# Six weight slabs of the forgetting attention split in halves ahead of time, and the relative bias written per head

## The chip, the cores and the metric

The kernel runs on one core of one Trainium2 chip. The metric is device time in microseconds (us) of one execution. A core has a matrix engine (PE), a vector engine (DVE), an activation engine (ACT) and a general engine (POOL), a sync engine (SP) that issues most of its transfers in order, and 16 DMA engines that move data between the chip's DRAM and the on-chip buffers.

## The reference, cut to what matters

Two transformer blocks run over 512 tokens of width 1024, in float32.

```python
# block 1
h = rmsnorm(x, ln1); z = h @ w_in
y_pool = pool_mixer(u_pool)                 # trailing means, widths 2, 4, 8, 16
y_gla  = gla_mixer(gq, gk, gv, gg, ga)      # chunked gated linear attention, 4 heads
y_fox  = fox_mixer(fq, fk, fv, ff)          # softmax(q k^T/8 + F_t - F_s) v, causal, 8 heads
x = x + concat(y_pool, y_gla, y_fox) @ w_o
x = x + (silu(h2 @ w_gate) * (h2 @ w_up)) @ w_down     # h2 = rmsnorm(x, ln2), inner width 2816
x = rmsnorm(x, ln_f)
# block 2
h = rmsnorm(x, norm_g); q_lat, c_kv, ..., z_a, z_b, gate_a, gate_b = split(h @ w_in)
y_a = mla_attention(...) * silu(z_a)        # latent attention, 8 heads
y_b = dsa_attention(...) * silu(z_b)        # top-128 keys of an index score, bias by relative position
x = x + (sigmoid(gate_a) * (y_a @ w_o_a) + sigmoid(gate_b) * (y_b @ w_o_b)) @ w_out
return rmsnorm(x, final_g)
```

## The kernel before

**Number format.** Every float32 operand of a product is kept as a high part and a low part in the matrix engine's rounded float32. `split` makes the two: ACT copies the operand with rounding into hi (L189), and DVE or POOL subtracts hi from it into lo (L191). A product is three matmuls into one bank: hi by hi, hi by lo, lo by hi.

**Weights.** A slab is a 128x1024 weight tile of 512 KB. `weight` loads it raw into tag `wr` (2 buffers) on SP's queue (L199) and splits it into tags `wh` and `wl` (3 buffers each). The lo of a slab goes to POOL or to DVE by `self.share`: with 1 all go to POOL, with 2 every second one. `ready` gives a slab: if it has been stored before in split form, it loads hi and lo from DRAM and no engine works on it; otherwise it calls `weight`.

**Stages and their times in the trace.** Linear attention with pooling and the first projections (`gla_phase`) runs from about 24 to 129 us. Forgetting attention (`fox_phase`) with the first half of `w_o` runs from 129 to about 217, and the second half of `w_o` to 242. The MLP has two halves of eleven gate/up steps and eight down steps each: gate/up 242 to 364, down 364 to 428, gate/up 428 to 553, down 553 to 614. Block 2 has its index and latent projections from 614, the latent attention from 680 to 797, the sparse attention to 982, then the output projections to 1050.

**Order.** The order of PE's work is written by hand in the program. A planner (`spawn`, `later`, `go`, `need`) keeps a clock of PE's work, counted as moving columns at 2.4 per ns. A thread yields the time until it wants to run again, and work that was put off with `later` (projections, `w_o`) fills the time between. The other engines run their own instructions in order, and so does SP's queue: a transfer that waits holds back those behind it.

**Linear attention.** Temporaries [128x512] come from tag `b` with 18 buffers, which are given out in turn. `gla_phase` uses them for its chains and for `pooling` (the `nx` tiles, L780 to L793), and the forgetting attention uses them for q and k (L815, L817), the split stacks of a head (`stacks`, L342 to L349) and the scores. Head 0 makes four tiles for its stacks and its output before its first score.

**Forgetting attention.** Pairs of heads p = 0 to 3 need the slabs fq p and fk p of `w1s`. The products `w_o` of half 0 need slabs `w1o` 0 to 3. All of these pass through `weight`.

**MLP.** The gate/up weights come through `weight`. Beside them, `store` takes one slab of block 2 per step from the list `ahead`: raw load into `sr` (2 buffers, L252), hi on ACT into `sh` (1 buffer), lo on POOL into `sl` (1 buffer), and two stores to DRAM (L259). `down` loads its weights as 704 KB tiles `wd` (2 buffers, L906) and splits them on ACT and DVE. `store` runs in every gate/up step from the second on and in the odd down steps. `relative` makes the relative bias in down steps 0 and 1 of half 0: two small matmuls, eight rows `gd` to DRAM, and one transfer of 2560 KB (L890) that writes each head's 640 values 128 times, each row one element further on. Block 2 reads it as the shear tensor, head by head.

**Block 2.** `attention` divides a score row by its sum either on DVE (L406, for the query blocks in `norm`) or on ACT (L408). For the sparse attention `norm` is `NDSA`. `merge_a(m)` loads 256 KB of gate_a into a buffer of tag `z` (3 buffers, L1254), multiplies it with the product (L1258) and sends it to DRAM tile `ma` from POOL's queue (L1215); gate_b uses the same tag.

Of the kernel before, what the change touches and what calls it, by code (L numbers as in the profile page):

```python
# [11 lines left out]
F32 = mybir.dt.float32  # L12
F32R = mybir.dt.float32r
# [7 lines left out]
P = 128  # L21
T = 512
D = 1024
KD = D // P
# [9 lines left out]
XR = 7  # L34
XO = 4
RSW = 800
LSW = 3000
RRW = 3300
KTW = 800
# [39 lines left out]
NS = 3  # L79
NFOX = (1, 3)  # L80
NMLA = ()
NDSA = (0,)
UNIT = 5120.0


class Body:
# [109 lines left out]

    def weight(self, src, n=1024, pool=None):
        raw = self.wp.tile([P, 1024], F32, tag="wr", name="wr", bufs=WR)
        self.nc.sync.dma_start(raw[:, :n], src)  # L199
        hi = self.wp.tile([P, 1024], F32R, tag="wh", name="wh", bufs=3)  # L200
        lo = self.wp.tile([P, 1024], F32R, tag="wl", name="wl", bufs=3)
        self.nw += 1
        if pool is None:
            pool = self.nw % self.share == 0
        self.split(hi[:, :n], lo[:, :n], raw[:, :n], self.nc.gpsimd if pool else self.nc.vector)
        return hi, lo
# [31 lines left out]
    def ready(self, name, i, n=1024):  # L238

        if (name, i) not in self.stored:  # L240
            return self.weight(self.A[name][i], n)
        out = []
        for tag, src in zip(("wh", "wl"), self.stored[name, i]):
            out.append(self.wp.tile([P, 1024], F32R, tag=tag, name=tag, bufs=3))
            self.nc.sync.dma_start(out[-1][:, :n].bitcast(F32), src)
        return out

    def store(self, pool, name, i, n=1024):

        nc = self.nc  # L250
        raw = pool.tile([P, 1024], F32, tag="sr", name="sr", bufs=2)[:, :n]
        nc.sync.dma_start(raw, self.A[name][i])  # L252
        hi, lo = (pool.tile([P, 1024], F32R, tag=t, name=t, bufs=1)[:, :n] for t in ("sh", "sl"))
        with self.tc.issue_after(self.last_split):
            self.split(hi, lo, raw, nc.gpsimd)
        self.stored[name, i] = kept = []
        for part, src in (("h", hi), ("l", lo)):
            kept.append(self.dp.tile([P, n], F32, name=f"{part}_{name}_{i}"))
            nc.sync.dma_start(kept[-1], src.bitcast(F32))  # L259

    def token_major(self, act, t, w):

# [314 lines left out]
    def w_o(self, mix, m, half):  # L577
        x = self.x[m]
        if m % 2 == 0:
            self.w_pair = self.weight(self.A["w1o"][half * 4 + m // 2])  # L580
        ps = yield from self.dense(self.w_pair, mix[4 * half:4 * half + 4], kt=4, w0=(m % 2) * 512)
        self.nc.vector.tensor_tensor(x, ps, x, op=OP.add)

    def gla_phase(self, ctx, h, R, Rc, mix, mp, b, fd, psg, held, V, proj):
        nc, A = self.nc, self.A
# [187 lines left out]
        def pooling(f):  # L773
# [22 lines left out]
            self.mm(ps, wpool[:, f, :], nx)  # L796
            self.split_scaled(mix[f][0], mix[f][1], ps, self.gain("pool_scale", f))

        self.spawn(chain(0, held))
        self.later("gv", gla_v(), 2 * UNIT)  # L800
        self.spawn(chain(1), CH1)
# [72 lines left out]
    def relative(self, pool):  # L874

        nc = self.nc
        relb = self.const(pool, "relb", [32, 8])
        onehot = self.const(pool, "onehot", [32, 640])
        shear = self.shear = self.dp.tile([8, P * 641], F32, name="shear")
        gd = self.dp.tile([8, 640], F32, name="gd")  # L880
        g8 = pool.tile([8, 640], F32, name="g8")
        yield
        for c in range(0, 640, 320):
            ps = self.bank("tr")
            self.mm(ps[:8, :320], relb, onehot[:, c:c + 320])
            nc.scalar.activation(g8[:, c:c + 320], ps[:8, :320], AF.Copy, scale=-1.0)
        nc.sync.dma_start(gd, g8)

        dst = bass.AP(tensor=shear.tensor, offset=shear.offset, ap=[[P * 641, 8], [641, P], [1, 640]])
        nc.sync.dma_start(dst, bass.AP(tensor=gd.tensor, offset=gd.offset, ap=[[640, 8], [0, P], [1, 640]]))  # L890
        yield

    def mlp(self, ctx):
        nc, A, x = self.nc, self.A, self.x
        fp = self.pool(ctx, "ff")
        wd = self.pool(ctx, "wd")
        act = [tuple(fp.tile([P, T], F32R, name=f"f{c}{k}") for c in "hl") for k in range(FH)]
        lng = fp.tile([P, KD], F32, name="lng")
        o, o2 = GAINS["ln_f"][0], GAINS["norm_g"][0]
        nc.vector.tensor_tensor(lng, self.gains[:, o:o + KD], self.gains[:, o2:o2 + KD], op=OP.mult)  # L900
        ft = lambda tag: fp.tile([P, T], F32, tag=tag, name=tag, bufs=2)
        self.res = self.dp.tile([T, D], F32, name="res")

        def down(m, half):
            raw = wd.tile([P, FH * P], F32, tag="wd", name="wd", bufs=2)
            nc.sync.dma_start(raw, A["w1d"][half * KD + m])  # L906
            hi, lo = (wd.tile([P, FH * P], F32R, tag=t, name=t, bufs=2) for t in ("wdh", "wdl"))
            self.split(hi, lo, raw)
            return hi, lo

        def turn(m):

            s, o = ft("g"), ft("u")
            nc.scalar.activation(s, x[m], AF.Identity, scale=self.gain("ln_f", m))
            yield
            tr = self.bank("tr")
            for t in range(NT):
                self.tp(tr[:, t * P:(t + 1) * P], s[:, t * P:(t + 1) * P])
            nc.scalar.activation(o, tr, AF.Copy)
            nc.sync.dma_start(self.res[:, m * P:(m + 1) * P].rearrange("(t p) c -> p t c", p=P),  # L920
                              o.rearrange("p (t c) -> p t c", c=P))

        t2 = lambda name, a, b: [("w2s", T2[name] + i, 1024) for i in range(a, b)]
        ahead = [("w2m", 0, KD * 72)] + t2("c_kv", 0, 2) + t2("q_idx", 0, 2) + t2("q_lat", 0, 3) + [("w2kv_v", 0, 1024)]
        ahead += t2("gate_b", 0, 8) + [("w2uq_r", 0, 768), ("w2pair", 0, 640)]
        for p in range(4):
            ahead += t2("gate_a", 2 * p, 2 * p + 2 if p < 2 else 4) + t2("z_a", p, min(p + 1, 3))
            ahead += [("w2pair", p + 1, 640)] if p < 2 else []
        ahead = deque(ahead)
        relative = self.relative(wd)  # L930
        turns = []
        for half in range(2):
            for k in range(FH):
                m = half * FH + k
                if m == 0:
                    self.entry()
                ps = self.first.pop(0) if self.first else self.all(self.dense(self.slab("w1gu", 2 * m), self.h))
                gen = None if self.first else self.dense(self.slab("w1gu", 2 * m + 1), self.h)
                g = ft("g")
                nc.vector.tensor_tensor(g, ps, self.R2, op=OP.mult)  # L940
                nc.scalar.activation(g, g, AF.Silu)
                ps = self.first.pop(0) if gen is None else self.all(gen)
                u = ft("u")
                nc.vector.tensor_tensor(u, ps, self.R2, op=OP.mult)  # L944
                nc.vector.tensor_tensor(u, u, g, op=OP.mult)
                self.split(act[k][0], act[k][1], u)
                if m and ahead:
                    self.store(wd, *ahead.popleft())
            for m in range(KD):
                ps = self.all(self.dense(down(m, half), act, kt=FH))  # L950
                if m % 2 and ahead:
                    self.store(wd, *ahead.popleft())
                if half == 0 and m < 2:
                    next(relative)
                nc.vector.tensor_tensor(x[m], ps, x[m], op=OP.add)  # L955
                if half == 1:
                    if m == 0:
                        h = self.acts()
                        s1, s2 = self.sums(), self.sums()
                    self.split_scaled(h[m][0], h[m][1], x[m], lng[:, m:m + 1])  # L960
                    eng = nc.vector if m == KD - 1 else nc.gpsimd
                    self.square_into(s1, x[m], m == 0, eng=eng)
                    self.square_into(s2, x[m], m == 0, scale=self.gain("ln_f", m), eng=eng)
                    for g in turns:
                        self.all(g)
                    turns = [turn(m)]
                    next(turns[0])
        self.s1, self.s2 = [s1], [s2]
        self.h, self.turns = h, turns
# [25 lines left out]
    def block2(self, ctx, psm, psc):  # L995
# [254 lines left out]
        wa = {}  # L1250

        def merge_a(m):
            g = at("z", 3)
            nc.sync.dma_start(g, kept["gate_a", m])  # L1254
            if m % 2 == 0:
                wa[0] = self.weight(A["w2oa"][m // 2])
# [297 lines left out]
```

## Time and profile before

| | |
|---|---|
| median of 3 runs | 1057.81 us (1057.36 to 1058.91) |
| profiled execution, its time | 1059.3 us |
| its span in the profile | 1057.4 us |
| PE busy | 1038.4 us, 98% |
| DVE, ACT, POOL busy | 641.7, 548.1, 371.2 us |
| PE's granted clock | 0.999 of 2.4 GHz |

The span runs from the first to the last instruction, and 1.9 us of the profiled execution's time lie around it. PE's busy time is what matmuls occupy by the profile; their ends are modelled.

### The profile page before, as it was taken

The page shows a single profiled execution, that of the slowest core. Times are in us where ns is not written, and L with a number is a line of the kernel's source. Part 1 is how long each engine was busy: PE and PEld are TensorE (multiplying, and loading weights), DVE is VectorE, ACT ScalarE, POOL GpSimd, SP SyncE. Part 2 cuts the span into 40 slices and gives each one's busy share as a digit, 9 for nine tenths or more (in the row PEclk, how much of TensorE's full clock was granted, in tenths as well). Part 3 has the DMA queues.
Part 4 walks back from the last instruction along what each step waited for, and adds up shares of the span by engine and source line. Part 5 has one row for each costly group of instructions (what it writes and reads, how often), then busy time and mean ns, then how long its engine had stood idle before and what let it go on. Part 6 is the DMA issues. An engine that isn't in the chain of part 4 may idle for free.

```text
span 1057.4 us, 14279 instructions
## 1 busy us (share of the span) xinstructions
PE 1038.4 (98%) x5264; PEld 862.3 (82%) x5264; DVE 641.7 (61%) x1141; ACT 548.1 (52%) x956; POOL 371.2 (35%) x213
## 2 busy tenths in 40 slices
PE   9999999999999999999999999999999999999997
PEld 6888977788888877888888888888887898888786
DVE  6573488866554522445434435799995656787652
ACT  7673578745433322243325545655565657677333
POOL 1243322133454522255433411100023346665354
PEclk9999999999999999999999999999999999999999
DMA  6222132226677588466776344564532323435842
GB/s 224 90 81 81 60 100 71 71 80 223 202 242 254 200 286 275 159 224 217 247 255 223 106 146 160 178 214 163 175 126 100 100 71 120 130 100 162 285 141 80
DMA packets 57822, 169.78 MB, mean 161 GB/s; under 512 B 6744, under 2 KB 11240, under 8 KB 57752
## 3 DMA queue, kind: packets, MB, share of 16 engines
q1 hardware_dynamic: 54664, 162.54, 45.9%
q10 hardware_dynamic: 2448, 4.22, 1.1%
q0 software_dynamic: 640, 2.10, 0.5%
q8 instruction: 42, 0.69, 0.3%
q14 instruction: 28, 0.23, 0.1%
HBM read 130.86 MB, written 40.60 MB: 162 GB/s over the span
## 4 chain that ended last, share of the span: by engine, by line
PE 54%; DMA 4%; ACT 2%; DVE 2%; issue 1%; SPq 1%; POOL 1%; DVEq 0%; POOLq 0%; ACTq 0%
PE mm L152 45%; PE sc L152 4%; PE pv L152 2%; PE tr L159 2%; DMA wd<-in_w1d 1%; PE tr L152 1%; DMA ma<-z 1%; SPq L252 1%; DMA l_w2s<-sl 1%; POOL sl L191 1%; DMA z<-gate_a 0%; DMA wl<-l_w2s 0%; DVE kst L191 0%; DVE qst L343 0%; ACT s L403 0%
## 5 line engine op out<-in xcount | busy, mean ns | idle before, releaser
L152 PE MATMUL mm<-hh,wh 128*128 128x512 f32 (+2 forms) x808 | 322.5, 399 | 0.2
L191 POOL TENSOR_TENSOR wl<-wr,wh 128x1024 fp32r<-128x1024 f32 (+1 forms) x78 | 195.2, 2504 | 362.6 <-ACT wh L189 340.0
L152 PE MATMUL mm<-hl,wh 128*128 128x512 f32 (+3 forms) x808 | 314.7, 389 | 0.9 <-DVE hl L527 0.9
L152 PE MATMUL mm<-hh,wl 128*128 128x512 f32 (+1 forms) x800 | 312.0, 390 | 0.0
L189 ACT ACTIVATE wh<-wr 128x1024 fp32r<-128x1024 f32 (+2 forms) x114 | 118.8, 1043 | 174.4 <-PE mm L152 145.9
L152 PEld LDWEIGHTS mm<-hh,wh 128*128 128x128 f32 (+1 forms) x808 | 152.0, 188 | 30.9 <-issue 1.3
L152 PEld LDWEIGHTS mm<-hh,wl 128*128 128x128 f32 (+1 forms) x800 | 149.8, 187 | 32.0
L152 PEld LDWEIGHTS mm<-hl,wh 128*128 128x128 f32 (+2 forms) x808 | 151.3, 187 | 29.4 <-DVE hl L527 2.2
L191 POOL TENSOR_TENSOR sl<-sr,sh 128x1024 fp32r<-128x1024 f32 (+3 forms) x28 | 73.3, 2617 | 72.3 <-ACT sh L189 46.0
L152 PE MATMUL mm<-fh,wdh 128*128 128x512 f32 x176 | 70.3, 400 | 0.9 <-ACT wdh L189 0.9
L152 PE MATMUL mm<-fh,wdl 128*128 128x512 f32 x176 | 69.7, 396 | 0.9 <-DVE wdl L191 0.9
L152 PE MATMUL mm<-fl,wdh 128*128 128x512 f32 x176 | 69.6, 395 | 0.0
L944 DVE TENSOR_TENSOR u<-mm,R 128x512 f32<-128x512 f32 x22 | 15.2, 691 | 67.2 <-PE mm L152 67.2
L189 ACT ACTIVATE wdh<-wd 128x1408 fp32r<-128x1408 f32 x16 | 22.1, 1380 | 62.4 <-PE mm L152 41.1
L419 DVE TENSOR_TENSOR pl<-tr,ph 128x128 fp32r<-128x128 f32 (+1 forms) x96 | 45.9, 483 | 11.6 <-ACT ph L418 10.3
L403 ACT ACTIVATE s<-s,m 128x128 f32<-128x128 f32 (+1 forms) x64 | 35.8, 559 | 29.6 <-DVE m L401 29.3
L191 DVE TENSOR_TENSOR fl<-u,fh 128x512 fp32r<-128x512 f32 x22 | 40.9, 1861 | 14.7 <-ACT fh L189 14.7
L191 DVE TENSOR_TENSOR wl<-wr,wh 128x1024 fp32r<-128x1024 f32 (+1 forms) x35 | 42.9, 1226 | 11.2 <-ACT wh L189 10.9
L955 DVE TENSOR_TENSOR x<-mm,x 128x512 f32<-128x512 f32 x16 | 11.1, 691 | 63.6 <-PE mm L152 63.6
L330 POOL TENSOR_TENSOR ss<-ss,t 128x512 f32<-128x512 f32 x21 | 29.7, 1428 | 53.4 <-ACT t L329 41.6
L152 PE MATMUL mm<-wh,hh 128*128 128x256 f32 x160 | 46.5, 291 | 0.0
L418 ACT ACTIVATE ph<-tr 128x128 fp32r<-128x128 f32 (+1 forms) x96 | 40.4, 426 | 11.6 <-PE tr L159 10.5
(343 smaller groups left out, 2057.1 us busy)
## 6 DMA issues: line engine op xcount, KB each, us to landing
wr<-in_w1gu SPq DMA_DIRECT2D x44, 512.0 KB, 4.3
sr<-in_w2s SPq DMA_DIRECT2D x22, 512.0 KB, 5.5
wd<-in_w1d SPq DMA_DIRECT2D x16, 704.0 KB, 5.8
h_w2s<-sh SPq DMA_DIRECT2D x22, 512.0 KB, 2.9
l_w2s<-sl SPq DMA_DIRECT2D x22, 512.0 KB, 3.2
wh<-h_w2s SPq DMA_DIRECT2D x22, 512.0 KB, 3.7
wl<-l_w2s SPq DMA_DIRECT2D x22, 512.0 KB, 4.8
wr<-in_w2s SPq DMA_DIRECT2D x17, 512.0 KB, 3.5
```

Of the source, the lines that this page charges most:

```text
L152: self.nc.tensor.matmul(out, l, r, start=start, stop=stop)
L159: self.nc.tensor.transpose(out, src, self.ident if ident is None else ident)
L189: last = self.nc.scalar.activation(hi, src, AF.Copy)
L191: (eng or self.nc.vector).tensor_tensor(lo, src, hi.bitcast(F32), op=OP.subtract)
L252: nc.sync.dma_start(raw, self.A[name][i])
L330: return (eng or nc.gpsimd).tensor_tensor(ssum, ssum, sq, op=OP.add)
L403: nc.scalar.activation(s[:, :n], s[:, :n], AF.Exp, scale=-1.0, bias=m[:, 0:1], accum_out=m[:, 1:2])
L418: nc.scalar.activation(hi, trv, AF.Copy)
L419: nc.vector.tensor_tensor(lo, trv, hi.bitcast(F32), op=OP.subtract)
L944: nc.vector.tensor_tensor(u, ps, self.R2, op=OP.mult)
L955: nc.vector.tensor_tensor(x[m], ps, x[m], op=OP.add)
```

## The change

- `store_part` and a thread `ahead` in `gla_phase`: the slabs fq 3 and fk 3 of `w1s` and 0 to 3 of `w1o` are loaded in halves of 128x512 into buffers of tag `b`, split on ACT and DVE, and stored in DRAM as hi and lo. The thread starts 52 us of planner time after the stage's start and yields 3.5 us after each half.
- `stored` now keeps a list of column ranges, each with its hi and lo. `ready` loads each range, so such a slab comes by four transfers of 256 KB. `w_o` uses `ready`.
- `relative` is stretched over gate/up steps 0 to 9 of half 0. The 2560 KB transfer becomes eight of 320 KB, one in each of the steps 2 to 9, each issued after the latest raw weight load.
- In half 0 a slab is stored after every down step, and the list of slabs to store grows from 28 to 31 (gate_a 4, z_a 3, the fourth `w2pair`).
- `NDSA` becomes empty, so eight 128x128 divisions go from DVE to ACT.
- `merge_a` takes its gate_a tile for m = 6 and 7 from tag `lat` (10 buffers).

```diff
@@ -34,6 +34,8 @@
 XR = 7
 XO = 4
 RSW = 800
+STB = 52000
+STP = 3500
 LSW = 3000
 RRW = 3300
 KTW = 800
@@ -79,7 +81,7 @@
 NS = 3
 NFOX = (1, 3)
 NMLA = ()
-NDSA = (0,)
+NDSA = ()
 UNIT = 5120.0
 
 
@@ -196,7 +198,8 @@
 
     def weight(self, src, n=1024, pool=None):
         raw = self.wp.tile([P, 1024], F32, tag="wr", name="wr", bufs=WR)
-        self.nc.sync.dma_start(raw[:, :n], src)
+        last = self.nc.sync.dma_start(raw[:, :n], src)
+        self.last_load = getattr(last, "ins", last)
         hi = self.wp.tile([P, 1024], F32R, tag="wh", name="wh", bufs=3)
         lo = self.wp.tile([P, 1024], F32R, tag="wl", name="wl", bufs=3)
         self.nw += 1
@@ -239,11 +242,23 @@
 
         if (name, i) not in self.stored:
             return self.weight(self.A[name][i], n)
-        out = []
-        for tag, src in zip(("wh", "wl"), self.stored[name, i]):
-            out.append(self.wp.tile([P, 1024], F32R, tag=tag, name=tag, bufs=3))
-            self.nc.sync.dma_start(out[-1][:, :n].bitcast(F32), src)
+        out = [self.wp.tile([P, 1024], F32R, tag=tag, name=tag, bufs=3) for tag in ("wh", "wl")]
+        for c, *parts in self.stored[name, i]:
+            for t, src in zip(out, parts):
+                self.nc.sync.dma_start(t[:, c].bitcast(F32), src)
         return out
+
+    def store_part(self, new, name, i, c, eng):
+
+        nc, n = self.nc, c.stop - c.start
+        raw, hi, lo = new(F32)[:, :n], new(F32R)[:, :n], new(F32R)[:, :n]
+        nc.sync.dma_start(raw, self.A[name][i][:, c])
+        self.split(hi, lo, raw, eng)
+        parts = []
+        for p, src in (("h", hi), ("l", lo)):
+            parts.append(self.dp.tile([P, n], F32, name=f"{p}_{name}_{i}_{c.start}"))
+            nc.sync.dma_start(parts[-1], src.bitcast(F32))
+        self.stored.setdefault((name, i), []).append((c, *parts))
 
     def store(self, pool, name, i, n=1024):
 
@@ -253,10 +268,11 @@
         hi, lo = (pool.tile([P, 1024], F32R, tag=t, name=t, bufs=1)[:, :n] for t in ("sh", "sl"))
         with self.tc.issue_after(self.last_split):
             self.split(hi, lo, raw, nc.gpsimd)
-        self.stored[name, i] = kept = []
+        kept = []
         for part, src in (("h", hi), ("l", lo)):
             kept.append(self.dp.tile([P, n], F32, name=f"{part}_{name}_{i}"))
             nc.sync.dma_start(kept[-1], src.bitcast(F32))
+        self.stored[name, i] = [(slice(0, n), *kept)]
 
     def token_major(self, act, t, w):
 
@@ -577,7 +593,7 @@
     def w_o(self, mix, m, half):
         x = self.x[m]
         if m % 2 == 0:
-            self.w_pair = self.weight(self.A["w1o"][half * 4 + m // 2])
+            self.w_pair = self.ready("w1o", half * 4 + m // 2)
         ps = yield from self.dense(self.w_pair, mix[4 * half:4 * half + 4], kt=4, w0=(m % 2) * 512)
         self.nc.vector.tensor_tensor(x, ps, x, op=OP.add)
 
@@ -796,6 +812,14 @@
             self.mm(ps, wpool[:, f, :], nx)
             self.split_scaled(mix[f][0], mix[f][1], ps, self.gain("pool_scale", f))
 
+        def ahead():
+
+            for name, i in [("w1s", T1["fq"] + 3), ("w1s", T1["fk"] + 3)] + [("w1o", j) for j in range(4)]:
+                for c in range(0, D, T):
+                    self.store_part(b, name, i, slice(c, c + T), nc.vector)
+                    yield STP
+
+        self.spawn(ahead(), STB)
         self.spawn(chain(0, held))
         self.later("gv", gla_v(), 2 * UNIT)
         self.spawn(chain(1), CH1)
@@ -886,9 +910,11 @@
             nc.scalar.activation(g8[:, c:c + 320], ps[:8, :320], AF.Copy, scale=-1.0)
         nc.sync.dma_start(gd, g8)
 
-        dst = bass.AP(tensor=shear.tensor, offset=shear.offset, ap=[[P * 641, 8], [641, P], [1, 640]])
-        nc.sync.dma_start(dst, bass.AP(tensor=gd.tensor, offset=gd.offset, ap=[[640, 8], [0, P], [1, 640]]))
-        yield
+        for hd in range(8):
+            yield
+            dst = bass.AP(tensor=shear.tensor, offset=shear.offset + hd * P * 641, ap=[[641, P], [1, 640]])
+            with self.tc.issue_after(self.last_load):
+                nc.sync.dma_start(dst, bass.AP(tensor=gd.tensor, offset=gd.offset + hd * 640, ap=[[0, P], [1, 640]]))
 
     def mlp(self, ctx):
         nc, A, x = self.nc, self.A, self.x
@@ -924,8 +950,8 @@
         ahead = [("w2m", 0, KD * 72)] + t2("c_kv", 0, 2) + t2("q_idx", 0, 2) + t2("q_lat", 0, 3) + [("w2kv_v", 0, 1024)]
         ahead += t2("gate_b", 0, 8) + [("w2uq_r", 0, 768), ("w2pair", 0, 640)]
         for p in range(4):
-            ahead += t2("gate_a", 2 * p, 2 * p + 2 if p < 2 else 4) + t2("z_a", p, min(p + 1, 3))
-            ahead += [("w2pair", p + 1, 640)] if p < 2 else []
+            ahead += t2("gate_a", 2 * p, 2 * p + 2 if p < 2 else 5) + t2("z_a", p, p + 1)
+            ahead += [("w2pair", p + 1, 640)] if p < 3 else []
         ahead = deque(ahead)
         relative = self.relative(wd)
         turns = []
@@ -946,12 +972,12 @@
                 self.split(act[k][0], act[k][1], u)
                 if m and ahead:
                     self.store(wd, *ahead.popleft())
+                if m < 10:
+                    next(relative, None)
             for m in range(KD):
                 ps = self.all(self.dense(down(m, half), act, kt=FH))
-                if m % 2 and ahead:
+                if (m % 2 or half == 0) and ahead:
                     self.store(wd, *ahead.popleft())
-                if half == 0 and m < 2:
-                    next(relative)
                 nc.vector.tensor_tensor(x[m], ps, x[m], op=OP.add)
                 if half == 1:
                     if m == 0:
@@ -1250,7 +1276,7 @@
         wa = {}
 
         def merge_a(m):
-            g = at("z", 3)
+            g = at("lat", 10, dt=F32R).bitcast(F32) if m >= KD - 2 else at("z", 3)
             nc.sync.dma_start(g, kept["gate_a", m])
             if m % 2 == 0:
                 wa[0] = self.weight(A["w2oa"][m // 2])
```

## Rows read from the trace of the kernel before

**Rows 1.** Busy time on the page: us, share of the span, instructions.

```profile
PE 1038.4 (98%) x5264; PEld 862.3 (82%) x5264; DVE 641.7 (61%) x1141; ACT 548.1 (52%) x956; POOL 371.2 (35%) x213
```

**Rows 2.** Windows by stage: us, each engine's busy time, clock, DMA share, GB/s.

```profile
24.00:129.00 105.00, 104.69 (x685) 90.69 (x684) 55.69 (x78) 59.30 (x82) 34.33 (x29) 1.00 0.23 76
129.00:242.00 113.00, 110.49 (x601) 89.35 (x600) 91.85 (x201) 78.47 (x172) 34.21 (x17) 1.00 0.26 83
242.00:364.00 122.00, 122.00 (x546) 100.97 (x545) 63.37 (x62) 52.35 (x63) 55.49 (x21) 1.00 0.70 236
364.00:428.00 64.00, 62.13 (x264) 48.52 (x263) 20.23 (x17) 16.52 (x16) 15.83 (x6) 1.00 0.75 259
```

**Rows 3.** PE's waits: instruction, releaser, us in total, times, longest us.

```profile
PE tr L159 <- ACT s L408: 2.3, 1, 2.3
PE tr L159 <- DVE pl L419: 1.7, 3, 0.8
PE mm L152 <- DVE z L1258: 1.5, 1, 1.5
...
PE tr L159 <- DVE s L406: 1.1, 2, 0.6
...
PE mm L152 <- ACT wdh L189: 0.9, 1, 0.9
PE mm L152 <- DVE wdl L191: 0.9, 1, 0.9
```

**Rows 4.** Chain of waits in down of half 0: start us, us, what.

```profile
387.13 0.77 SPq L890
...
387.96 7.19 SPq L252
...
395.26 15.65 DMA wd<-in_w1d
...
411.01 1.39 ACT wdh L189
...
412.42 1.64 DVE wdl L191
```

**Rows 5.** Chain of waits at the last merge_a.

```profile
976.43 7.68 DMA ma<-z
...
984.13 4.38 DMA z<-gate_a
```

**Rows 6.** DMA issues in several stages: KB each, median us from issue to landing.

```profile
gate_a<-z ACTq DMA_DIRECT2D x8, 256.0 KB, 2.1
...
bias<-fd SPq DMA_DIRECT2D x7, 256.0 KB, 3.4
...
wr<-in_w1s SPq DMA_DIRECT2D x10, 512.0 KB, 3.5
...
wd<-in_w1d SPq DMA_DIRECT2D x7, 704.0 KB, 5.9
```

**Rows 7.** Groups by line, 24 to 129 or 129 to 242: us, ns each.

```profile
L189 ACT ACTIVATE mh<-b 128x512 fp32r<-128x512 f32 x2 | 1.3, 631 | 0.6 <-DVE b L756 0.5
...
L673 DVE TENSOR_TENSOR b<-gx,b 128x512 f32<-128x512 f32 x8 | 5.1, 687 | 0.1
...
L191 POOL TENSOR_TENSOR wl<-wr,wh 128x1024 fp32r<-128x1024 f32 x12 | 28.9, 2416 | 79.7 <-ACT wh L189 61.5 <-PE tr L159 9.3 <-issue 8.9
...
L343 DVE TENSOR_TENSOR b<-b 64x512 fp32r<-64x512 f32 x7 | 11.2, 1595 | 0.4
```

**Rows 8.** Timeline around the first score: start us, us, instruction.

```profile
84.33 0.33 SPq L199 DMA_DIRECT2D wr<-in_w1s  x1
...
103.08 0.60 POOL L789 COPY b<-b 64x512 f32<-64x512 f32 x1
...
114.15 0.61 ACT L342 ACTIVATE b<-b 64x512 fp32r<-64x512 f32 x1
...
129.52 0.22 PE L152 MATMUL sc<-b 128*128 128x128 f32 x1
```

## The prediction

> **What bounds the kernel now.** The page comes first: PE is busy for 98% of the span [rows 1], so a change can win only where PE stands still, or where PE work is taken away. The diff takes no matmul away and adds none. The windows by stage say where PE stands still [rows 2]: 113.00 - 110.49 = 2.51 us in the forgetting attention, 64.00 - 62.13 = 1.87 in down of half 0, 0.31 in the linear attention and nothing in gate/up of half 0. PE's waits name what it waits for [rows 3]: the score path's DVE and ACT work, twice a split of a down weight (0.9 and 0.9), once `merge_a`'s product (1.5). The chain of waits tells how the last two come about. In down, one SP entry follows another from the shear transfer at 387.13, `sr` holds the queue for 7.19, and the `wd` tile issued at 395.26 lands 15.65 us later [rows 4] where the median is 5.9 [rows 6]. In the last `merge_a`, gate_a's load waits 7.68 us for an older `ma<-z` to leave the buffer and then takes 4.38 [rows 5].
>
> **Terms of the sum.** They are made against the profiled execution, 1059.3 us (span 1057.4 and 1.9 around it). That is 1.5 above the median of the runs, so what comes out is lowered by 1.5.
>
> **1. Shear in eight parts.** Removed is one transfer that lies ahead of two `wd` tiles on the same DMA engines. Both waits of down follow from the late tile [rows 3, 4], with 1.87 us of idle PE together [rows 2]. I take -1.9; the bounds are 0, if another tile becomes late there, and -1.9. The eight parts run beside gate/up, where PE has no idle time and DMA moves 236 GB/s at a share of 0.70 [rows 2]. Their 2.6 MB in 122 us make it about 257 GB/s, still under the 259 of the down window. Each costs SP one issue of about 0.33 us, the price of a weight load's [rows 8]; placed after the latest raw load it does not hold that load back. The two small matmuls and the copies only change place: 0.
>
> **2. `merge_a` from `lat`.** Its last two loads no longer wait for a `z` buffer. -1.5, the wait in [rows 3]; bounds 0 and -1.6 (the wait with the restart of the pipeline).
>
> **3. Forgetting attention without six splits.** ACT loses six copies of some 1.05 us each (twice the 631 ns of a half-size one, less its overhead) and POOL six subtractions of 2.416 us [rows 7], 14.5 us; SP issues four loads for one. DVE is the busiest after PE there, 91.85 of 113 us [rows 2], and its `stacks` subtraction over 64x512 takes 1595 ns in the mean where one over 128x512 took 687 in the stage before [rows 7]; I read that as time lost beside POOL's subtractions. Quieter POOL and ACT shorten the score path that PE waits for. I take -1.5 of the 2.51 us idle. Bounds: -2.5, and +1, because some 3.2 us of the planner's filler (the rest of the second value projection) moves into the linear attention and leaves 6% less cover between the scores (51.2 for 54.4 us by its count).
>
> **4. The twelve halves in the linear attention.** Removed: nothing. Added per half: a load of 256 KB, 0.63 us of ACT, 0.69 of DVE (the 687 ns row), two stores of 256 KB [rows 7]; in all 7.6 us of ACT, 8.2 of DVE, 36 SP issues of 0.33 us = 12, and 9.4 MB of traffic. ACT is busy for 59.30 and DVE for 55.69 of 105 us there, DMA for 0.23 [rows 2], so as work it is covered. What can show is its order. The kernel's planner counts 87.9 us for the stage from its start to what is now its end, about 99 in the trace (24 to 123), so 1.126 us of trace for one of its own. The halves then stand at 24 + 52 x 1.126 = 82.6 us and every 3.94 us after it, the last at 125.9. Each needs three tiles of `b`, and the first score stands behind all of them, since head 0's stacks are handed `b` tiles last. PE's list also grows ahead of the first score by the moved filler, so PE comes to it at about 129.5 + 2.9 = 132.4 us [rows 8].
> How long one half takes: a 256 KB transfer lies between 2.1 (gate_a's store) and 3.4 us (the bias load), 512 KB take 3.5 in this stretch [rows 6]. I take 3.0, nearer the load. SP runs in order: if a half's load stands behind the hi store of the half before, the cycle is 0.33 + 3.0 + 0.63 + some 0.2 of hand-overs = 4.2 us, over the pace of 3.94 by 0.26. The last half's hi is then ready at 125.9 + 4.2 + eight times 0.26 = 132.2 (the eight that come after `pooling`'s last tiles). Two copies on ACT and a subtraction on DVE make the stacks, about 1.9 us with the 0.61 of [rows 8], so 134.1: PE waits 1.7 us. I take +1.7. Bounds: 0 with the 2.1 us transfer (cycle 3.3, no lag), and +10 (below).
> The Trainium skill, "DMA: Bandwidth & Descriptors", section "Anatomy of one DMA — SWDGE (gpsimd) path", gives a fixed 2.0 us and bytes at 436 GB/s for a transfer. By it, as an estimate, a half-slab would take 2.6 us, the cycle would be 3.8, there would be no lag, and the sum would be lower by 1.7, 1052.9, inside the forecast's own range. Its section "Rules for kernel authors" wants 1 MiB or more in a transfer, which speaks against halves; at a DMA share of 0.23 [rows 2] the stage lacks no bandwidth, and if a half cost as much as the whole slab's 3.5 us [rows 6], the sum would be the slow end of the first rival below.
>
> **5. The rest.** Three more slabs are stored, four more store steps in down of half 0. Each store moves 1.5 MB: 16.6 MB of that window (64 us at 259 GB/s [rows 2]) lose 2.6 and gain 6.3, 20.3 in all or 317 GB/s, against 296 for a steady step of one `wd` and one store in 7.75 us. I take 0; if the tiles come late, 0.3 us in each of eight steps, +2.4. In block 2 three slabs lose their split: 0, or the 2.3 us wait of [rows 3] if it hangs on POOL's backlog. Eight divisions on ACT for DVE: two waits of 1.1 us in all end at DVE's L406 [rows 3]; ACT would be waited for instead. 0, bounds -0.5 and +0.5.
>
> **The sum:** 1.7 - 1.5 - 1.9 - 1.5 = -3.2 us. 1059.3 - 3.2 = 1056.1, and 1.5 lower, on the median, 1054.6.
>
> **The rivals.**
> *A chain of halves makes the first score late (no change, or slower).* The last `nx` tile of `pooling` begins at 103.08 [rows 8]. If `b` tiles are given out strictly in the order of the program, only four halves come before that, and eight follow one by one: 103.1 + 8 x 4.2 = 136.7, with the stacks 138.6, so PE waits 138.6 - 132.4 = 6.2 us. With the rest: +6.2 - 4.9 = +1.3, 1059.1. It decides where the cycle is longer than (132.4 - 1.9 - 103.1)/8 = 3.4 us. For it: `b` is one ring, and head 0's stacks begin at 114.15 in the trace, 15.4 us before their use, a slack that the halves spend. Against it: the loads may run ahead of the stores, DMA and ACT being mostly idle. With the 3.5 us load the cycle is 4.7 and the wait 10.2: +5.3, 1063.1.
> *Each load stands behind both stores of the half before (slower).* DVE's 0.69 and an issue of 0.33 join the cycle: 5.2 us, 103.1 + 41.6 + 1.9 = 146.6, a wait of 14.2, +9.3, 1067. The same rows speak for and against; on SP the lo store would have to be queued first.
> *Everything that waits goes away:* no lag, -2.5 in the forgetting attention, -2.3 in block 2: -8.2, 1049.6. Against it, DVE's load on the score path does not go down but for its stretch.
> *Down of half 0 stays bound by its transfers:* `wd` late as now (no -1.9) or +2.4, so 1056.5 to 1058.9. For it: the 317 GB/s. Against: gate/up runs at 236 with no idle PE.
> *It doesn't do what it says:* the two stalls are met by something else that ends at the same time (the last `merge_a` by gate_b's loads on the same queue, down by `sr`), and the fox stage keeps its waits: 1057.8.
>
> **How the numbers follow.** The smallest difference that a measurement of this kernel can tell is about 0.2%, 2.1 us. Chances: the forecast 0.38, whose own range is 1052.0 to 1055.7; all waits gone 0.07; the chain of halves 0.36, of which 0.04 faster, 0.20 within 0.2% and 0.12 slower (its cycle between 3.4 and 4.7 us); both stores 0.09; down bound by transfers 0.06; nothing done 0.04. Faster: 0.38 + 0.07 + 0.04 = 0.49. Same: 0.20 + 0.06 + 0.04 = 0.30. Slower: 0.12 + 0.09 = 0.21. The range leaves out both stores, half of all waits gone and the upper third of the slower part of the chain, about 0.17: 1050.8 to 1061.5.
>
> **What would show it.** In the profile after: PE's first score at 132 to 134 and no long wait ahead of it (the chain of halves: a wait of 3 us or more there, ending at a `b` tile of the stacks, and SP's loads of `w1s` halves 4.2 us apart); less than 1.5 us of idle PE in the forgetting attention; no wait on `wdh` or `wdl` in down of half 0, with `wd` landing in under 8 us; no wait on L1258. The prediction is wrong if the halves are not done when PE comes to its first score, and by as much as they are late.

## The result and the profile after

The changed kernel takes 1069.50 us in the median (1068.79 to 1070.40, 4 runs), the kernel before 1057.59 beside it: a ratio of 1.0118, 95% interval [1.0104, 1.0131], 11.9 us slower. Forecast were 1054.6, with 1061.5 as the upper end. In the profiled executions the span went from 1057.4 to 1067.0.

PE's work is the same, 5264 matmuls. The line of the page with the busy times, to be held against [rows 1]:

```profile
PE 1039.3 (97%) x5264; PEld 864.6 (81%) x5264; DVE 636.0 (60%) x1145; ACT 552.9 (52%) x970; POOL 358.5 (34%) x207
```

The windows by stage answer to [rows 2]; down of half 0 lies about 11 us later than before, so its window is 374 to 438.

```profile
24.00:129.00 105.00, 104.81 (x684) 90.75 (x684) 56.65 (x83) 59.79 (x83) 33.27 (x29) 1.00 0.41 137
129.00:242.00 113.00, 97.83 (x539) 80.02 (x539) 77.99 (x198) 73.30 (x164) 11.25 (x6) 0.94 0.38 125
...
242.00:364.00 122.00, 122.00 (x545) 99.99 (x544) 68.61 (x67) 55.38 (x69) 58.64 (x25) 1.00 0.70 238
374.00:438.00 64.00, 64.00 (x277) 51.67 (x276) 23.53 (x19) 21.23 (x20) 24.85 (x11) 1.00 0.87 301
```

Down of half 0 has no idle PE any more, though its transfers went from 259 to 301 GB/s. The loss stands in one place: between 129 and 242 PE is idle for 15.2 us instead of 2.51, and the granted clock there is 0.94. PE's waits, against [rows 3]:

```profile
PE sc L154 <- DVE b L359: 13.1, 1, 13.1
PE tr L161 <- ACT s L424: 2.5, 2, 2.3
PE mm L154 <- DVE ml L193: 1.7, 1, 1.7
...
PE tr L161 <- DVE pl L435: 0.2, 1, 0.2
```

The waits on the down weights, on `merge_a`'s product and on L406's division are gone, and the forgetting attention's waits on `pl` fell from 1.7 to 0.2. New are 13.1 us ahead of the first score and 1.7 us on an `ml`. The chain of waits ahead of the first score (start us, us, what):

```profile
106.05 0.61 ACT b L191
106.68 0.33 SPq L260
107.05 2.91 DMA b<-in_w1o
109.98 0.64 ACT b L191
...
120.04 5.07 DMA b<-in_w1o
125.19 0.64 ACT b L191
125.85 0.32 SPq L260
...
126.22 3.07 DMA b<-in_w1o
129.38 0.64 ACT b L191
130.03 0.32 SPq L260
...
134.59 4.07 DMA b<-in_w1o
138.68 0.64 ACT b L191
139.34 0.32 SPq L260
...
143.64 0.62 ACT b L358
...
145.09 0.69 DVE b L359
```

Read a round of it: a half lands, ACT copies its hi (0.64), SP issues the store of that hi (0.32), only then the next half's load goes out, and 2.9 to 5.1 us later it lands. Nine halves pass like that from 100.83, where the first of them is asked for, to 143.73, 4.77 us each. L358 and L359, the stacks of head 0, come behind the last, L358 directly behind its copy in ACT's order. PE's last matmul ahead of the score ends at 132.8, and the score starts at 145.92.

That the chain of nine starts as late as 100.83 is seen on SP (its timeline):

```profile
92.84 0.33 SPq L201 DMA_DIRECT2D wr<-in_w1fv  x1
100.44 0.33 SPq L201 DMA_DIRECT2D wr<-in_w1s  x1
100.83 0.42 SPq L255 DMA_DIRECT2D b<-in_w1s  x1
```

A raw slab's load (L201) stands ahead of the half's load (L255) in SP's order. It waits 7.2 us for its buffer, until POOL has made the lo of an earlier slab, and SP issues nothing from 93.17 to 100.44.

The wait costs more than its length. The windows around it (us, busy time of each engine, then the granted clock):

```profile
132.00:146.00 14.00, 0.92 (x5) 0.48 (x3) 3.56 (x6) 5.16 (x9) 4.11 (x2) 0.70 0.84 289
146.00:150.00 4.00, 3.82 (x11) 3.00 (x11) 2.33 (x6) 3.40 (x7) 0.00 (x0) 0.50 0.03 13
150.00:154.00 4.00, 4.00 (x20) 3.14 (x18) 1.52 (x6) 1.31 (x4) 0.00 (x0) 0.85 0.00 0
154.00:158.00 4.00, 4.00 (x23) 3.19 (x22) 2.53 (x8) 2.45 (x7) 0.00 (x0) 1.00 0.51 140
```

For 4 us after the wait PE runs at 0.50, the lower of its two levels (1.2 GHz), and for part of the next 4: 4 x 0.50 + 4 x 0.15 = 2.6 us of work at full clock are lost. Together 15.7 us.

### The profile page after: what moved, and what is told of

It is laid out like the page before. It is cut to its first block, busy times and chain, and to the rows that moved or that the text cites. A ratio compares the mean times of both kernels' runs of the same rounds, so it can differ in the third digit from the quotient of the medians.

```text
span 1067.0 us, 14417 instructions
## 1 busy us (share of the span) xinstructions
PE 1039.3 (97%) x5264; PEld 864.6 (81%) x5264; DVE 636.0 (60%) x1145; ACT 552.9 (52%) x970; POOL 358.5 (34%) x207
## 4 chain that ended last, share of the span: by engine, by line
PE 86%; DVE 5%; ACT 5%; DMA 3%; issue 1%; SPq 0%; ACTq 0%; DVEq 0%
PE mm L154 72%; PE sc L154 5%; PE pv L154 4%; PE tr L161 3%; DMA b<-in_w1o 2%; PE tr L154 2%; ACT wh L191 1%; ACT b L191 0%; DMA x<-in_xT 0%; DMA wr<-in_w1s 0%; DVE kst L193 0%; DVE qst L359 0%; DVE b L689 0%; ACT s L419 0%; DVE lat L193 0%
## 5 line engine op out<-in xcount | busy, mean ns | idle before, releaser
L193 POOL TENSOR_TENSOR wl<-wr,wh 128x1024 fp32r<-128x1024 f32 x69 | 175.6, 2545 | 378.1 <-ACT wh L191 367.8
L191 ACT ACTIVATE wh<-wr 128x1024 fp32r<-128x1024 f32 (+1 forms) x105 | 109.7, 1045 | 171.8 <-PE mm L154 146.9
L193 POOL TENSOR_TENSOR sl<-sr,sh 128x1024 fp32r<-128x1024 f32 (+3 forms) x31 | 80.5, 2596 | 61.1 <-DMA l_w2s<-sl 25.4
L970 DVE TENSOR_TENSOR u<-mm,R 128x512 f32<-128x512 f32 x22 | 15.2, 691 | 67.2 <-PE mm L154 67.2
L419 ACT ACTIVATE s<-s,m 128x128 f32<-128x128 f32 (+1 forms) x64 | 35.8, 559 | 30.6 <-DVE m L417 28.8
L191 ACT ACTIVATE sh<-sr 128x1024 fp32r<-128x1024 f32 (+3 forms) x31 | 30.7, 990 | 36.3 <-DMA h_w2s<-sh 32.8
L424 ACT ACTIVATE s<-s,m 128x128 f32<-128x128 f32 (+1 forms) x64 | 35.6, 557 | 24.6 <-DVE m L420 24.4
```

Of the source, the lines that this page charges most:

```text
L191: last = self.nc.scalar.activation(hi, src, AF.Copy)
L193: (eng or self.nc.vector).tensor_tensor(lo, src, hi.bitcast(F32), op=OP.subtract)
L419: nc.scalar.activation(s[:, :n], s[:, :n], AF.Exp, scale=-1.0, bias=m[:, 0:1], accum_out=m[:, 1:2])
L424: nc.scalar.activation(s[:, :n], s[:, :n], AF.Copy, scale=m[:, 2:3])
```

## The experiments

The theory: the halves are one chain through the ring of `b` tiles, each load behind the hi store of the half before, and head 0's stacks are behind all of them; everything else in the change is a small gain. The rival: the loss hangs on the amount of added work and traffic, or on another part of the change, and only shows at the first score. Ratios are to the kernel before, run beside each, with their 95% intervals.

**Without the halves** (`e1`).

```diff
-        self.spawn(ahead(), STB)
```

> The changed kernel without the thread that splits the twelve halves; the six slabs come raw and are split where they are used, everything else of the change stays. Theory (the halves' chain through the ring of b tiles makes the first score late: 13.1 us of wait and some 2.6 us of half clock after it): the wait ahead of the first score is gone and the gains of the shear (-1.9) and of merge_a (-1.5) stand alone, 1054.2. Rival (the loss comes from another part of the change and the late score only absorbs it): 1060 or more.

Measured: 1056.14 us, ratio 0.9977 [0.9967, 0.9986], -2.4 us. The first score waits for nothing. The old waits of the forgetting attention on `pl` are back as they were:

```profile
PE tr L161 <- DVE pl L435: 1.7, 3, 0.8
```

The thread is the whole loss, and the rest of the change a gain, a little under the -3.4 expected (its interval reaches to -3.5). That doesn't yet tell chain from amount.

**The next load ahead of the split** (`e2`).

```diff
...
+    raw = self.load_part(b, *halves[0])
+    for j, half in enumerate(halves):
+        this, raw = raw, self.load_part(b, *halves[j + 1]) if j + 1 < len(halves) else None
+        self.store_part(b, *half, nc.vector, this)    # split, two stores
         yield STP
```

> The changed kernel with the same twelve halves at the same places, from the same b tiles; only the raw load of the next half is requested ahead of the split of this one. Theory (the cycle is one load behind the hi store of the half before, because the next raw tile is handed out only after this half's lo tile): the load leaves the cycle, the halves keep their pace of 3.9 us, the wait at the first score falls below 2 us and the time to 1052 to 1056. Rival (too few b tiles, or too much work for ACT, DVE and the DMA engines in the linear attention): the wait stays above 8 us, 1064 to 1070.

Measured: 1057.82 us, ratio 1.0002 [0.9987, 1.0018]. The same halves, tiles, splits and stores, and 11.7 us are back. The last half's copy starts at 126.97 instead of 143.10 (timeline of ACT), with single loads that are slower than in the changed kernel (4.7 us in the median for 3.2), two of them under way at once:

```profile
126.97 0.63 ACT L191 ACTIVATE b<-b 128x512 fp32r<-128x512 f32 x1 [0.30 <-DMA b<-in_w1o]
```

So it is the order of the load and not the amount. The wait at the first score is gone, but two others stand in the stage (PE's waits, 129 to 242):

```profile
PE tr L161 <- ACT b L429: 2.9, 1, 2.9
PE mm L154 <- DVE ml L193: 1.7, 1, 1.7
```

The first begins at 138.1, behind the first score, and costs clock too (0.54 from 140.6 to 144.0): the raw slabs' splits and head 1's stacks are still crowded behind the late end of the chain.

**An earlier start, the load order unchanged** (`e6`).

```diff
-STB = 52000
+STB = 20000
```

> The changed kernel with the thread's start at 20 instead of 52 us of planner time. Theory: eleven or twelve halves come before pooling's last tiles, so the first score finds its stacks; what the chain delays is now the linear attention's own tiles, up to some us of wait between 60 and 110: 1053 to 1060. Rival (the amount): 1066 to 1070.

Measured: 1066.34 us, ratio 1.0076 [1.0051, 1.0100], outside what I had written for the theory and inside the range of its rival, the amount; the time alone would speak for the rival. The trace speaks against it. There is no wait at the first score, but the linear attention's own work stands behind the halves now, and PE waits there:

```profile
PE sc L154 <- ACT b L715: 9.5, 1, 9.5
```

The chain of waits ahead of it is again loads of halves with a copy and a store between them; L715, the linear attention's copy of `kt`, comes behind a half's copy in ACT's order:

```profile
66.00 5.45 DMA b<-in_w1s
71.47 0.64 ACT b L191
72.13 0.33 SPq L260
...
72.55 3.33 DMA b<-in_w1s
...
80.56 0.63 ACT b L191
81.18 0.49 ACT b L715
```

A place earlier moves the wait and doesn't remove it. What this run also shows: from 150 to 242 PE has no idle time at all, so the stored slabs can take the whole of the forgetting attention's waits away.

**Tiles of their own** (`e3`): three tiles of a new tag for the halves, and 15 `b` tiles instead of 18, for want of room.

```diff
-NB = 18
+NB = 15
+        hb = lambda dt=F32: mp.tile([P, T], dt, tag="hb", name="hb", bufs=3)
-                    self.store_part(b, name, i, slice(c, c + T), nc.vector)
+                    self.store_part(hb, name, i, slice(c, c + T), nc.vector)
```

> The changed kernel with three tiles of a tag of their own for the halves and 15 instead of 18 b tiles for the rest (there is no room for both). Theory: the chain still runs one half after the other, some 5 us each, but head 0's stacks don't stand behind it, so there is no wait at the first score: 1052 to 1056. Rival (the amount of work and traffic): 1064 to 1070. Should 15 b tiles be too few, short waits appear in the forgetting attention.

Measured: 1068.41 us, ratio 1.0082 [1.0045, 1.0119], with runs from 1061.85 to 1072.06. A miss, and in time inside the rival's range again. The edit changed more than the tiles: the first half's load goes out at 14.28 us and the last at 84.05, for 71.00 and 139.71 in the changed kernel, with the same start on the planner's clock. So that the wait at the first score is gone, as expected, doesn't show that the ring alone had made it. One of 4.0 us has come in the linear attention. The chain of waits there:

```profile
62.30 3.18 DMA hb<-in_w1o
...
65.59 0.12 ACT hb L191
...
66.23 1.28 ACT L700
...
67.53 0.21 ACT dec L700
67.75 0.95 ACT wh L191
...
68.72 1.23 DVE wl L193
69.95 1.90 DVE b L689 x4
```

A half's copy stands in ACT's order ahead of the linear attention's own L700 and waits there for its load. So the ring is not the only way in which a half can hold others: an instruction that waits for a load holds its engine. The trace is of the run of 1061.85 us, so it shows only part of the median's loss. How much of it the three missing `b` tiles have, and why the runs differ by 10 us, I haven't separated.

**Fewer halves** (`e10`, `e11`): the changed kernel with five and with four slabs in the thread.

```diff
-for name, i in [("w1s", T1["fq"] + 3), ("w1s", T1["fk"] + 3)] + [("w1o", j) for j in range(4)]:
+for name, i in [("w1s", T1["fq"] + 3), ("w1s", T1["fk"] + 3)] + [("w1o", j) for j in range(3)]:   # e11: range(2)
```

> The changed kernel with five slabs instead of six in the thread (ten halves; w1o 3 comes raw as before). Theory: each half after pooling's last tile lengthens the chain by its cycle, 4.77 us as the changed kernel's trace has it, so two fewer take 9.5 us off the wait of 13.1: 3 to 4 us of wait at the first score, some of the half clock still behind it, 1058 to 1061. Rival (the loss hangs on the split slabs being used, not on the chain's length): one sixth of it goes, 1067.

> The changed kernel with four slabs in the thread (eight halves; w1o 2 and 3 come raw as before). Theory: the chain ends some 5 us before PE comes to the first score, so no wait is left there: 1054 to 1056. Rival: two sixths of the loss go, 1065.

Measured: 1061.71 us, ratio 1.0051 [1.0036, 1.0066], and 1056.84 us, ratio 0.9998 [0.9984, 1.0012]; both lie a little over the range expected. The wait of the run with five slabs:

```profile
PE sc L154 <- ACT b L364: 3.7, 1, 3.7
```

13.1 with six slabs, 3.7 with five, none at the first score with four: two halves are worth 9.4 us, twice a cycle of 4.7, until the slack is used. The run with five slabs also waits 1.7 us on L966 in the MLP, which the changed kernel doesn't. With four slabs there is a wait at 135.2 like the one that the second experiment had at 138.1, behind the chain's end:

```profile
PE tr L161 <- ACT b L424: 2.5, 1, 2.5
```

**The shear and `merge_a` each alone** (`e4`, `e5`): the kernel before with that part of the diff and nothing else.

```diff
+        for hd in range(8):                # e4: eight transfers, in gate/up steps 2 to 9
+            yield
+            ...
-            g = at("z", 3)                 # e5
+            g = at("lat", 10, dt=F32R).bitcast(F32) if m >= KD - 2 else at("z", 3)
```

> The kernel before with the relative bias written per head, one transfer in each of eight gate/up steps; nothing else of the change. Theory: the late down tile and both waits of 0.9 us on its split are gone, nothing is late in gate/up: -1.9 us. Rival (the eight transfers hold back weight loads in gate/up, or another down tile is late): 0 to +2.

> The kernel before with the gate_a tiles of the last two merge_a taken from the other tag; nothing else of the change. Theory: the wait of 1.5 us on the product is gone, -1.5 us. Rival (the load is held back in SP's queue by something else, or the loads it now runs beside arrive later): the wait stays or moves, 0.

Measured: 1055.81 us, ratio 0.9984 [0.9973, 0.9994], -1.7 us; and 1056.80 us, ratio 0.9988 [0.9979, 0.9997], -1.3 us. The window of down in the first, with no idle PE at 222 GB/s:

```profile
364.00:428.00 64.00, 64.00 (x276) 51.62 (x275) 21.48 (x19) 17.51 (x15) 16.22 (x6) 1.00 0.63 222
```

In the second the wait on the product is gone. It is not of one size, though: the first run, which doesn't touch `merge_a`, has 0.6 us there for the 1.5 of [rows 3].

**The load order mended and the start earlier** (`e7` at 45.5 us, `e8` at 40 us of planner time, both otherwise as `e2`).

```diff
-STB = 52000
+STB = 45500     # e8: 40000
```

> The second experiment (next raw load ahead of the split) with the thread started at 45.5 instead of 52 us of planner time, so that it ends inside the linear attention and draws no filler out of the forgetting attention. Theory (what is left of the second experiment's waits, 2.9 us behind the late end of the chain and 1.7 us at the end of w_o for want of filler, comes from where the thread ends): both go, the forgetting attention has under 0.5 us of idle PE, 1057.9 - 1.9 - 1.5 - 2.2 = 1052.3. Rival (those waits belong to the stored slabs' loads or to the new order of ACT and DVE): they stay, 1056 to 1058.

> As the one before, with the start at 40 us of planner time. Theory: the same 1052.3 if the halves' first tiles don't stand before the linear attention's own (its scores and states run to about 75 us of the trace); if they do, a wait of up to 2 us there and 1054. Rival: as the second experiment, 1056 to 1058.

Measured: 1054.12 us, ratio 0.9967 [0.9955, 0.9980], and 1054.79 us, ratio 0.9970 [0.9959, 0.9981]. Both are about 2 us above the 1052.3 expected. The wait of 2.9 us falls to 0.7 at 45.5 and is gone at 40 (where 0.6 us have come in the linear attention), so it was the late end of the chain. The 1.7 us on `ml` stay in both. I had them come from the moved filler, and these two runs don't test that: ahead of its first score PE has 789 matmuls at 45.5 and 783 at 40, for 774 in the kernel before and 789 in the changed one, so filler is moved here too. The timelines of POOL and DVE in the run at 40 show what makes the subtraction late:

```profile
217.47 2.37 POOL L193 TENSOR_TENSOR wl<-wr,wh 128x1024 fp32r<-128x1024 f32 x1 [14.55 <-ACT wh L191]
...
217.94 2.44 DVE L193 TENSOR_TENSOR ml<-b,mh 128x512 fp32r<-128x512 f32 x1
```

The subtraction that PE waits for takes 2.44 us beside POOL's, for 0.69 elsewhere. The Trainium skill, "GPSIMD Engine Reference", section "Key points", says that POOL shares its interfaces to the on-chip buffers with DVE, with contention where a DVE instruction has two inputs there; these two rows agree with it. The traces side by side say the same: in the five runs with this wait (the changed kernel, `e2`, `e3`, `e7`, `e8`) the last heads' subtraction takes 2.44 or 2.45 us beside POOL's, in the kernel before and the seven others 0.68 or 0.69. What brings the two together is open, and the moved filler isn't ruled out: `e6` and `e11`, with 774 matmuls ahead of the first score again, have no wait on `ml`, and `e10`, with 789, has 0.6 us.

**The other engine for that slab's lo** (`e9`): `e8` with the four lo parts of the second half of `w_o` changed over between POOL and DVE.

```diff
+                if m == 0:
+                    self.nw += 1
                 self.all(self.w_o(mix, m, 1))
+                if m == KD - 2:
+                    self.nw += 1
```

> The experiment with the next raw load ahead of the split and the start at 40 us, with the lo parts of the four w_o slabs of the second half changed over between POOL and DVE. Theory (the wait of 1.7 us on the last heads' lo part comes from a slab's lo on POOL that runs beside it and stretches the 0.69 us subtraction to 2.45): the wait falls below 0.7 us, about 1 us less, 1053.6. Rival (it comes from the slab's hi copy that stands ahead of it on ACT): the wait stays or grows, since the slab's lo now stands on DVE too, 1054 to 1056.

Measured: 1054.01 us, ratio 0.9969 [0.9959, 0.9978]. The wait falls from 1.7 to 0.8, nearly as expected; the slab's lo now stands ahead on DVE (1.22 us), and the subtraction itself is back at 0.69:

```profile
217.25 1.22 DVE L193 TENSOR_TENSOR wl<-wr,wh 128x1024 fp32r<-128x1024 f32 x1
218.38 0.69 DVE L193 TENSOR_TENSOR ml<-b,mh 128x512 fp32r<-128x512 f32 x1
```

The step in time is no larger than the intervals. This is the best version with `e7`: 3.3 us under the kernel before, 15 under the changed one, and PE is idle for 0.94 us between 129 and 242:

```profile
129.00:242.00 113.00, 112.06 (x612) 91.83 (x611) 84.50 (x203) 75.91 (x169) 19.95 (x11) 1.00 0.36 116
```

## Why the prediction was wrong, step by step

**Step 4, the halves, failed.** It took +1.7 us; the wait is 13.1, and 2.6 of clock are lost after it. What failed is that it placed the halves by the planner's clock, every 3.94 us from 82.6, with a lag of 0.26 for each of the last eight. The planner's clock alone doesn't place them: the first load went out at 71.00, and with the start 6.5 or 12 us earlier on the planner's clock (`e7`, `e8`) at 71.8 and 71.1. The fourth went out at 100.83, where the step has it at 94.4, behind the raw slab's load on SP. From there the pace is the cycle itself, 4.86 us from load to load, so the last load went out at 139.71 for 125.9: 13.8 us late, 6.4 of them from the fourth half's start and 7.4 from eight cycles.

The mechanism stood in the text as the first rival, with a wait of 6.2 us and a chance of 0.36, and its rows already told it: stacks with 15.4 us of slack behind a ring. The rival too was sized short, at three places. Nine halves follow one another and not eight. A cycle is 4.77 us and not 4.2, since loads took 2.9 to 5.1 us for the 3.0 assumed, and ACT had the linear attention's own work in between. The clock after the wait stood in no case. How much the ring itself does is not shown apart from the rest: a half's load waits for a buffer only once in the trace, for 0.5 us, and the run with tiles of their own moved the halves as well. What the runs show is the thread (`e1`), the order of the load (`e2`) and the number of halves (`e10`, `e11`).

**PE's arrival** was forecast at 132.4 and came at 132.8; **the order on SP** was read rightly: the load stands behind the hi store alone, so the rival with both stores falls, though its time of 1067 is the nearest of all to the measured one.

**The estimate from the page on transfers** (the Trainium skill, "DMA: Bandwidth & Descriptors", section "Anatomy of one DMA — SWDGE (gpsimd) path") of 2.6 us for a half-slab is under what was measured: the trace has a median of 3.2 in the changed kernel and of 4.7 with two under way. The page gives its figures for transfers that GpSimd issues, and these are on SP's queue.

**Step 1, the shear** (-1.9), measured alone -1.7: right. Gate/up moved 254 GB/s in that run, near the 257 worked out, with no idle PE. Down went to 301 GB/s with the added stores, near the 317 that were worked out, and no tile came late, so the rival of a down bound by its transfers falls as well.

**Step 2, `merge_a`** (-1.5), measured alone -1.3: right.

**Step 3, the forgetting attention** (-1.5): the mechanism was right. The waits on the score path went from 2.5 us to 0.2, and to nothing in several runs. In the changed kernel 1.7 of it are given back at the last `ml`, where a slab's lo on POOL runs beside it (POOL from 232.90, the subtraction from 233.37, 2.44 us); moving that lo took half of it away. Whether the moved filler, the bound of +1, has a part in bringing them together stays open.

**Step 5:** the two waits on L406 are gone, and one of 0.2 came on ACT's division; the wait of 2.3 us at the end of the latent attention stayed, as [rows 3] had it, so it doesn't hang on the three slabs that are stored now.

**The sum** of what the two profiles show is 13.1 + 2.6 - 1.9 - 1.5 - 0.4 (idle PE in the forgetting attention, 2.51 to 2.09 after the first score) - 0.9 (the waits on divisions, 3.4 to 2.5) = +11.0 us. It lies between the 9.6 of the two spans and the 11.9 of the medians. PE's busy time on the page can't confirm the 2.6: it rose by 0.9 us, and over the profiles of this case, all with 5264 matmuls, it lies between 1036.7 and 1041.4.

## What to carry to other kernels

When work is put into the shade of a stage, count its chain and not only its share of busy time: ACT, DVE and the DMA engines were less than 60% busy in the linear attention, and a chain of nine load, copy, store rounds at 4.77 us still ended 13 us late. An order in which a load waits behind the store of the piece before makes such a chain; to ask for the next load before splitting this piece took 11.7 us off with no other change. A start on the planner's clock doesn't say when the pieces run: look on SP's queue for what stands ahead of them. An added thread is placed by where its chain ends, and what stands behind it in each engine's order (the stacks, the linear attention's own tiles) tells how early it may begin.

## What the runs showed of the hardware

- PE's granted clock was lower after some waits, which cost work beyond them: after 13.1 us idle from 132.8 it was 0.50 for 4 us and 0.85 for the next 4; after 2.9 us idle in `e2` it was 0.54 over 3.4 us, and after 2.5 us in `e11` 0.64 over 4 us. After the 2.3 us at the end of the latent attention the profile before shows 1.00 in the next 3.3 us.
- Half-slab loads took 3.2 us in the median one at a time and 4.7 with two under way, each time beside the stores and the weight loads: as an estimate from the two medians, the second one brings (2 x 3.2)/4.7 = 1.4 times the loads in a time, not 2.
- The last heads' subtraction on DVE, over 128x512, took 2.44 or 2.45 us in the five runs where a subtraction of POOL over 128x1024 had begun some 0.5 us before it, and 0.68 or 0.69 in the eight others.
